# Mixing phases of a hybrid attention and linear-attention backbone: elementwise arithmetic moved from GpSimd to VectorE

## The chip, the cores and the metric

The kernel runs on one core of one Trainium2 chip, in one launch. The metric is the device time of the launch in microseconds (us); the median of a few executions counts. A core has TensorE for matmuls (PE in the profile, its weight loads PEld), VectorE (DVE), ScalarE (ACT), GpSimd (POOL) and SyncE (SP), which here issues all DMAs. Each engine works through its own instructions strictly in the order in which they stand in its queue, and waits on semaphores for the others. TensorE's clock has two levels, 1.2 and 2.4 GHz; the profile shows the granted clock as a share of the upper one.

## What is computed

Two layers over 512 latent tokens and 256 context tokens, width 1024, all in fp32. Cut to what matters here:

```python
h = modulate(rms_norm(x, g_norm1[l]), sh1, sc1)
aq, ak, av, gq, gk, gv, gr, ga, gate_a, gate_b = split_in(h @ w_in[l])
q = rope_2d(rms_norm(aq, q_gain[l]), row, col)      # 16 heads of 64
k = rope_2d(rms_norm(ak, k_gain[l]), row, col)      # 4 key heads
attn = window_attention(q, k, v, kc, vc, sink[l])   # windows of 128, plus all context keys
gf = log_sigmoid(ga @ w_decay + b_decay) / 16       # per direction, cumulated in chunks
o_l = bidir_gla(qg, kg, vg, gf, gb, s_f, s_b)       # 4 heads, decayed key-value states
gla = rms_norm(o_l, gla_gain[l]) * silu(gr)
y = sigmoid(gate_a) * (attn @ w_branch_attn[l]) + sigmoid(gate_b) * (gla @ w_branch_gla[l])
x = x + gt1 * (y @ w_out[l])
x = x + gt2 * squared_relu_mlp(modulate(rms_norm(x, g_norm2[l]), sh2, sc2), w_ff1[l], w_ff2[l])
```

The context tokens run through the same layer with their own modulation, except that the last layer needs no output of theirs.

## The kernel before

**Precision.** Each fp32 operand of a large product is split in two: `hi`, the operand rounded to the matmul type fp32r, and `lo`, the rest. Three matmuls (hi·hi, hi·lo, lo·hi) add up to the product. A split is two instructions: ScalarE makes `hi` (`act`, line 97), then some engine subtracts, `lo = src - hi` (`sub`, line 100). `unit` (line 147) does this for a block of weights that a DMA brought into `raw` (three buffers; `whi` and `wlo` have four each); `split` (line 140) does it for activations. Which engine subtracts is an argument, `lo_eng`, VectorE without it. The helpers `sub`, `mul` and `add` (lines 100, 103, 106) likewise take the engine as their last argument, so most elementwise work shows under these three lines, and only the tile names tell it apart.

**Stages of a layer.** `keys` (norm of the inputs, key and value projections, rotary turn, transposes), `attention`, `gla` (linear attention, four heads one after another), `merge` (gate times branch, added and split into `Y`), `project_out`, and then `mlp`, which the change does not touch. In the trace of before the first layer has its keys at about 65 to 112 us, attention to 480, linear attention to 942, merge to about 972, and the second layer from 1627, 1680, 1960 and 2296 us on.

**Attention.** For each of four groups of heads, each tile of 128 queries and each pair of heads: `queries` projects q into PSUM bank `mq`, normalises (`xn`), multiplies by the cosine and sine tables `rt` (products `r` and `u`, lines 373 and 374), adds and splits (`qh`); `scores` multiplies with the keys into PSUM tile `S`, of which there is one buffer; VectorE reads it with mask and maximum (`p`, `rmax`, line 453), then come the small steps `nm`, `es`, `den` (128x2 each), the exponential on ScalarE and the division of `p`; `values` transposes p (PSUM `pt`, three buffers, copied to `pT`), multiplies by v and splits the result into `ag`. Between these steps the loop puts the products of the merge gates (`gate`) and of the attention branch (`branch`), whose weights come through `unit`.

**Linear attention.** `decay` turns the low-rank product into cumulated decays (`az`, `mz`, a scan into `pf`, subtraction of the middle value `e`, exponentials into `E`); `gla_scan` multiplies keys and queries into `E` and carries the states `st`; `gla_read` makes the outputs, normalises and splits them into `G`. At each head's end `use` fetches the attention branch `ya` from DRAM (`yd`), multiplies it by its gate and sends it back.

**Merge.** `use` fetches gate `sb` and branch `ya` by DMA, computes `yb*sb`, adds `ya`, and splits the sum into `Y`, block by block of 512 or 256 tokens.

**What sets the order.** The program is recorded as it is written, and then a scheduler with a timeline model of its own sorts each engine's queue. The change alters costs and engines, so the scheduler sorts the queues anew, those of TensorE and SyncE too.

Of the kernel before, what the change touches and what calls it, by code (L numbers as in the profile page):

```python
# [59 lines left out]
class Net:  # L60
# [280 lines left out]
    def attn_consts(self, pool, l):  # L341

        nc = self.nc
        self.mask = pool.tile([128, 7, 128], F32, name="mask", bufs=1)
        nc.sync.dma_start(out=self.mask, in_=self.io["cst_mask"])
        rope = self.t2([128, SEQ // 128, 2, HD], "rope")
        nc.sync.dma_start(out=rope, in_=self.io["cst_rope"])
        self.rt = pool.tile([128, 2, SEQ // 128, 2, HD], F32, name="rt", bufs=1)
        for q in range(2):
            g = self.gains[:, q].rearrange("p (o d) -> p o d", o=1).to_broadcast([128, 2 * (SEQ // 128), HD])  # L350
            self.mul(self.rt[:, q].rearrange("p t s d -> p (t s) d"), rope.rearrange("p t s d -> p (t s) d"), g, nc.gpsimd)

    def qk_norm(self, pool, ps, q, t):
# [12 lines left out]
        if t >= SEQ // 128:  # L366
            g = self.gains[:, q].rearrange("p (o d) -> p o d", o=1).to_broadcast([128, 4, HD])
            self.mul(r, xn, g, nc.gpsimd)
            return r
        c = self.rt[:, q, t, 0].rearrange("p (o d) -> p o d", o=1).to_broadcast([128, 4, HD])  # L370
        s = self.rt[:, q, t, 1].rearrange("p (o d) -> p o d", o=1).to_broadcast([128, 4, HD])
        u = pool.tile([128, 4, HD], F32, name="u", tag="u", bufs=1)
        self.mul(r, xn, c, None if q else nc.gpsimd)
        self.mul(u, xn, s, nc.gpsimd if q else None)
        r8 = r.rearrange("p h (a b i) -> p (h a) b i", b=2, i=16)
# [4 lines left out]
    def keys(self, pool, H, us, uv, kT, v, late):  # L380
        nc = self.nc
        for t in CTXS.tiles + LAT.tiles:
            if t == LAT.tiles[0]:
                late()
            ps = self.mm()
            self.tm(ps[:, 0:256], us, H, t)
            r = self.qk_norm(pool, ps, 1, t)
            kd = [self.t2([128, NKV, 2, HD], "kd", F32R) for _ in range(2)]
            rb = r.rearrange("p h (o d) -> p h o d", o=1).to_broadcast([128, NKV, 2, HD])
            self.act(kd[0], rb, ACTF.Copy)  # L390
            self.sub(kd[1], rb, kd[0].bitcast(F32), nc.gpsimd)
            for s in range(2):
                pt = self.pt()
                for g in range(NKV):
                    nc.tensor.transpose(pt[:, g * 128:(g + 1) * 128],
                                        kd[s][:, g].rearrange("p o d -> p (o d)").bitcast(F32), self.ident)
                self.copy(kT[:, :, s, t * 128:(t + 1) * 128], pt.rearrange("p (g t) -> p g t", g=NKV), nc.scalar)
            ps = self.mm()
            self.tm(ps[:, 0:256], uv, H, t)
            self.copy(v[:, t], ps[:, 0:256], nc.scalar)  # L400
# [89 lines left out]
    def attention(self, pool, H, l, kT, v, ya, blocks, gate):  # L490
# [9 lines left out]
        def query(i):  # L500
            nonlocal us
            if i < len(steps):
                g, _, t, _ = steps[i]
                if t == tiles[0]:
                    us = self.panel(w, O_Q + g * 256, lo_eng=self.nc.gpsimd)
                qT[g, t] = self.queries(pool, H, us, t)
# [48 lines left out]

    def gate(self, H, l, off, j, n, sts, use, l0=False):

# [4 lines left out]
        else:  # L562
            src = w[:, c0:c0 + 128].rearrange("(k p) c -> p k c", p=128)
            us = [self.unit(lambda t: self.nc.sync.dma_start(out=t, in_=src), shape=(8, 128), lo_eng=None if l0 else self.nc.gpsimd)]
        for f in range(n):
# [9 lines left out]
    def attn_unit(self, l, g):  # L575
# [3 lines left out]
        def make(c):  # L579
            def loads(t):  # L580
                for s in range(2):
                    self.nc.sync.dma_start(out=t[s * 64:(s + 1) * 64], in_=w[s, :, :, c * 512:(c + 1) * 512])
            return self.unit(loads, shape=(2, 512), lo_eng=self.nc.gpsimd)
        return make
# [85 lines left out]
    def decay(self, st, pool, ga, hd, d, E):  # L670
# [11 lines left out]
        self.act(a, a, ACTF.Ln, bias=1.0)  # L682
        self.sub(m, m, a, nc.gpsimd)
        src, dst = (m, pf) if d == 0 else (m[:, ::-1], pf[:, ::-1])
# [5 lines left out]
        nc.vector.tensor_copy(out=e1, in_=p3[:, :, mid:mid + 1])  # L690
        self.sub(p3, p3, e1.to_broadcast([128, NT, 128]), nc.gpsimd)
        self.act(e2, p3[:, :, last:last + 1], ACTF.Exp, scale=1.0 / 16)
# [39 lines left out]
    def gla_scan(self, st, pool, E, ends, qs, ks, v, prev, full):  # L732
# [7 lines left out]
        for d in range(2):  # L740
            self.mul(E[:, d, 1, tt], ks[:, tt], E[:, d, 1, tt])
            if full:
                self.mul(E[:, d, 0, tt], qs[:, tt], E[:, d, 0, tt], nc.gpsimd)
        S = [{}, {}]
# [31 lines left out]
    def gla_read(self, st, pool, E, S, v, sg, G):  # L776
# [25 lines left out]
        for f in range(2):  # L802
            o = self.t2([128, st.T], "glo")
            self.mul(o, oT[:, f, :st.T], sg[f])
            self.split(G, o, (slice(None), f, slice(st.off, st.off + st.T)), nc.gpsimd)

    def gla(self, pool, H, l, E, yb, sts):
# [5 lines left out]
        def use(j, st, s):  # L813
            tt = slice(st.off, st.off + st.T)
            y = self.t2([128, st.T], "ya1")
            nc.sync.dma_start(out=y, in_=self.yd[:, j, tt])
            self.mul(y, y, s, nc.gpsimd)
            nc.sync.dma_start(out=self.yd[:, j, tt], in_=y)
# [66 lines left out]
    def merge(self, l, H, yb, Y, sts, pool):  # L885
        def use(j, st, s):
# [4 lines left out]
            self.mul(y, y, s)  # L891
            self.add(y, y, a, self.nc.gpsimd)
            self.split(Y, y, (slice(None), j, tt))
# [8 lines left out]
    def gate_early(self, H, l, sts):  # L902
        def keep(j, st, s):
            self.nc.sync.dma_start(out=self.gd[:, j, st.off:st.off + st.T], in_=s)
        return lambda j: self.gate(H, l, O_SB, j, 1, sts, keep, j < 3)

# [300 lines left out]
```

## Time and profile before

| what | value |
|---|---|
| median of three runs | 2745.8 us (2741.91 to 2748.45) |
| the profiled execution: its time | 2742.91 us |
| the profiled execution: span of the core | 2741.1 us |
| TensorE busy | 2579.2 us (94%) |
| weight loads busy | 2267.8 us (83%) |
| VectorE busy | 1634.7 us (60%), 3127 instructions |
| ScalarE busy | 1151.7 us (42%) |
| GpSimd busy | 780.1 us (28%), 574 instructions |
| mean granted clock of TensorE | 0.972 |

The busy times are unions of the instructions' intervals within the span. Matmuls are pipelined, so a busy TensorE is not one at its peak; what can be gained from it without changing its work is the time in which it sits idle, and the time in which it runs at the lower clock.

### The profile page before, as it was taken

What the parts mean: (1) busy time and instruction counts of PE and PEld (TensorE: products, weight loads), DVE (VectorE), ACT (ScalarE), POOL (GpSimd) and SP (SyncE); (2) the same over time, 40 slices, a digit from 0 to 9 for tenths busy, and PEclk for the clock granted to TensorE, in tenths of its full rate; (3) what the DMA queues carried; (4) which work ended last, traced back from release to release, by engine and by line L of the source; (5) the groups of instructions that cost most, each with busy time, mean ns of one, the idle gap of its engine ahead of it and who ended that gap; (6) DMA issues with size and microseconds to landing.
All of it is one profiled execution on the core that took longest, in us unless ns stands there. A gap on an engine that the chain in (4) does not pass through costs nothing. (4 is left out here: it accounts for less than half of the span.)

```text
span 2741.1 us, 43359 instructions
## 1 busy us (share of the span) xinstructions
PE 2579.2 (94%) x17227; PEld 2267.8 (83%) x17227; DVE 1634.7 (60%) x3127; ACT 1151.7 (42%) x2526; POOL 780.1 (28%) x574
## 2 busy tenths in 40 slices
PE   6899999999999898999999988999999998889999
PEld 3888887878878787888888988888888887879898
DVE  4566777534454468644455565787654446677765
ACT  3556554435252334322222245655445334434343
POOL 1413221211120214232223354233122112253444
PEclk7999999999999999999999999999999999999999
DMA  7212123233343433243333241222222225322333
GB/s 252 68 36 72 45 49 100 89 101 93 100 139 90 159 109 93 85 131 107 124 116 123 77 149 47 66 63 68 88 77 85 62 85 177 108 92 90 103 106 111
DMA packets 223838, 269.82 MB, mean 98 GB/s; under 512 B 18480, under 2 KB 185684, under 8 KB 223508
## 3 DMA queue, kind: packets, MB, share of 16 engines
q1 hardware_dynamic: 223636, 267.05, 32.0%
q8 instruction: 135, 2.21, 0.3%
q14 instruction: 67, 0.55, 0.1%
HBM read 244.21 MB, written 22.81 MB: 97 GB/s over the span
## 5 line engine op out<-in xcount | busy, mean ns | idle before, releaser
L97 ACT ACTIVATE whi<-raw 128x1024 fp32r<-128x1024 f32 (+1 forms) x350 | 333.0, 953 | 585.7 <-DMA raw<-in_w_ff 167.2
L920 PE MATMUL mm<-hid,whi 128*128 128x512 f32 (+1 forms) x1664 | 427.3, 347 | 21.0 <-ACT hid L97 10.1
L100 POOL TENSOR_TENSOR wlo<-raw,whi 128x1024 fp32r<-128x1024 f32 x126 | 306.1, 2434 | 321.4 <-ACT whi L97 295.4
L920 PEld LDWEIGHTS mm<-hid,whi 128*128 128x128 f32 x1664 | 290.5, 192 | 72.5 <-issue 11.9
L100 DVE TENSOR_TENSOR wlo<-raw,whi 128x1024 fp32r<-128x1024 f32 (+1 forms) x224 | 238.2, 1064 | 141.2 <-ACT whi L97 137.6
L920 PE MATMUL mm<-hid,wlo 128*128 128x256 f32 (+1 forms) x832 | 281.5, 343 | 0.0
L173 PE MATMUL mm<-H,whi 128*128 128x512 f32 (+1 forms) x760 | 263.0, 347 | 4.8 <-POOL H L100 4.3
L172 PE MATMUL mm<-H,whi 128*128 128x512 f32 (+1 forms) x760 | 264.0, 350 | 2.9 <-ACT H L97 2.1
L174 PE MATMUL mm<-H,wlo 128*128 128x512 f32 (+1 forms) x760 | 261.7, 345 | 0.0
L1065 DVE SCALAR_TENSOR_TENSOR x<-mm,mod,x 128x512 f32<-128x512 f32 (+1 forms) x208 | 126.6, 622 | 125.4 <-PE mm L920 125.1
L920 PE MATMUL mm<-H,whi 128*128 128x384 f32 (+1 forms) x896 | 197.6, 311 | 0.0
L100 POOL TENSOR_TENSOR hid<-c,hid 128x384 fp32r<-128x384 f32 (+1 forms) x112 | 112.4, 1013 | 248.3 <-ACT hid L97 244.0
L920 PEld LDWEIGHTS mm<-hid,wlo 128*128 128x128 f32 x832 | 158.8, 191 | 18.1
L173 PEld LDWEIGHTS mm<-H,whi 128*128 128x128 f32 x760 | 146.6, 193 | 21.0 <-POOL H L100 4.8
L172 PEld LDWEIGHTS mm<-H,whi 128*128 128x128 f32 x760 | 146.4, 194 | 19.9 <-ACT H L97 2.8
L174 PEld LDWEIGHTS mm<-H,wlo 128*128 128x128 f32 x760 | 146.5, 193 | 16.3 <-issue 0.2
L920 PEld LDWEIGHTS mm<-H,whi 128*128 128x128 f32 x896 | 149.8, 190 | 9.4 <-issue 4.9
L920 PE MATMUL mm<-T,whi 128*128 128x384 f32 (+1 forms) x672 | 145.2, 309 | 0.0
L920 PE MATMUL mm<-H,wlo 128*128 128x384 f32 (+1 forms) x448 | 137.5, 309 | 1.1 <-DVE wlo L100 1.1
L97 ACT ACTIVATE p<-p,nm 128x512 f32<-128x512 f32 (+1 forms) x128 | 98.1, 768 | 71.6 <-DVE nm L456 71.6
L453 DVE CUSTOM_DVE_ANT_0 p<-S,mask 128x512 f32<-128x512 f32 (+1 forms) x128 | 96.3, 752 | 46.3 <-PE S L451 44.5
L100 POOL TENSOR_TENSOR mz<-mz,az 128x256 f32<-128x256 f32 (+1 forms) x32 | 36.4, 1137 | 301.3 <-ACT az L97 189.5
(276 smaller groups left out, 6768.3 us busy)
## 6 DMA issues: line engine op xcount, KB each, us to landing
raw<-in_w_ff SPq DMA_DIRECT2D x136, 512.0 KB
raw<-in_w_mod SPq DMA_DIRECT2D x96, 512.0 KB
raw<-in_w_in SPq DMA_DIRECT2D x88, 512.0 KB
raw<-in_w_branch_attn SPq DMA_DIRECT2D x64, 256.0 KB
raw<-in_w_out SPq DMA_DIRECT2D x32, 512.0 KB
raw<-in_w_in SPq DMA_DIRECT2D x32, 256.0 KB
ya<-yd SPq DMA_DIRECT2D x32, 256.0 KB
raw<-in_w_branch_gla SPq DMA_DIRECT2D x16, 512.0 KB
```

The costliest lines, as they stand in the source:

```text
L97: return self.nc.scalar.activation(out=out, in_=in_, func=func, **kw)
L100: (eng or self.nc.vector).tensor_tensor(out=out, in0=a, in1=b, op=ALU.subtract)
L172: nc.tensor.matmul(ps[:, :n], lhsT=wh, rhs=xh, start=(i == 0), stop=False)
L173: nc.tensor.matmul(ps[:, :n], lhsT=wh, rhs=xl, start=False, stop=False)
L174: nc.tensor.matmul(ps[:, :n], lhsT=wl, rhs=xh, start=False, stop=(i == len(ks) - 1))
L453: nc.vector.tensor_tensor_reduce(out=p[:, :nk], in0=S[:, s0:s0 + nk], in1=mask, scale=1.0, scalar=-3e38, op0=ALU.add, op1=ALU.max, accum_o ...
L920: self.nc.tensor.matmul(ps[:, :n], lhsT=a, rhs=b, start=start and i == j == 0, stop=i == last and j == 2, skip_group_check=not start)
L1065: nc.vector.scalar_tensor_tensor(out=xx, in0=ps[:, :n], scalar=self.mod2[:, 5, j, c:c + 1], in1=xx, op0=ALU.mult, op1=ALU.add)
```

## The change

Fourteen places hand their elementwise arithmetic to VectorE instead of GpSimd: the rotary tables and products and the low part of the keys, the low parts of the attention's weight blocks (query panels, attention-branch units, and the gate blocks 3 to 5; gate blocks 0 to 2 were on VectorE already), in `decay` the subtractions on `mz` and `pf`, the product of queries and `E`, the low part of `G`, the product of `ya` and its gate, and the addition in `merge`. The arithmetic is the same. GpSimd keeps its memsets, the low parts of `H` in `norm`, and its work in `mlp`.

```diff
-            self.mul(self.rt[:, q].rearrange("p t s d -> p (t s) d"), rope.rearrange("p t s d -> p (t s) d"), g, nc.gpsimd)
+            self.mul(self.rt[:, q].rearrange("p t s d -> p (t s) d"), rope.rearrange("p t s d -> p (t s) d"), g)
...
-            self.mul(r, xn, g, nc.gpsimd)
+            self.mul(r, xn, g)
...
-        self.mul(r, xn, c, None if q else nc.gpsimd)
-        self.mul(u, xn, s, nc.gpsimd if q else None)
+        self.mul(r, xn, c)
+        self.mul(u, xn, s)
...
-            self.sub(kd[1], rb, kd[0].bitcast(F32), nc.gpsimd)
+            self.sub(kd[1], rb, kd[0].bitcast(F32))
...
-                    us = self.panel(w, O_Q + g * 256, lo_eng=self.nc.gpsimd)
+                    us = self.panel(w, O_Q + g * 256)
...
-            us = [self.unit(lambda t: self.nc.sync.dma_start(out=t, in_=src), shape=(8, 128), lo_eng=None if l0 else self.nc.gpsimd)]
+            us = [self.unit(lambda t: self.nc.sync.dma_start(out=t, in_=src), shape=(8, 128))]
...
-            return self.unit(loads, shape=(2, 512), lo_eng=self.nc.gpsimd)
+            return self.unit(loads, shape=(2, 512))
...
-        self.sub(m, m, a, nc.gpsimd)
+        self.sub(m, m, a)
...
-        self.sub(p3, p3, e1.to_broadcast([128, NT, 128]), nc.gpsimd)
+        self.sub(p3, p3, e1.to_broadcast([128, NT, 128]))
...
-                self.mul(E[:, d, 0, tt], qs[:, tt], E[:, d, 0, tt], nc.gpsimd)
+                self.mul(E[:, d, 0, tt], qs[:, tt], E[:, d, 0, tt])
...
-            self.split(G, o, (slice(None), f, slice(st.off, st.off + st.T)), nc.gpsimd)
+            self.split(G, o, (slice(None), f, slice(st.off, st.off + st.T)))
...
-            self.mul(y, y, s, nc.gpsimd)
+            self.mul(y, y, s)
...
-            self.add(y, y, a, self.nc.gpsimd)
+            self.add(y, y, a)
```

The argument `l0` of `gate`, by which `gate_early` told the first three gate blocks from the others, goes as well.

The queues are sorted anew. The first place is VectorE in the attention of layer 0, in a group of latent queries. Before, in its queue (`p` and `rmax` read `S`, `qh` is the low part of the queries, `ag` that of the attention's output):

```order
L112 COPY pT<-pt 128x512
L100 TENSOR_TENSOR qh<-r,qh 128x4x64
L453 ISA p,rmax<-S,mask 128x640
L453 ISA rmax 128x1
L100 TENSOR_TENSOR ag_2411<-pt,ag_2411 128x128
L456 SCALAR_TENSOR_TENSOR nm<-rmax,nsink 128x2
```

Now, at the same place:

```order
L112 COPY pT<-pt 128x512
L100 TENSOR_TENSOR wlo<-raw,whi 128x1024
L100 TENSOR_TENSOR qh<-r,qh 128x4x64
L453 ISA p,rmax<-S,mask 128x640
L453 ISA rmax 128x1
L100 TENSOR_TENSOR ag_2411<-pt,ag_2411 128x128
```

The low part of a weight block, `wlo`, now stands in VectorE's queue ahead of the queries' low part and of the reading of `S`; before, it stood in GpSimd's.

The second place is VectorE at the border of the first two heads of layer 0's linear attention (`E<-ks` belongs to the next head's scan, `ks` is its key projection taken out of PSUM). Before:

```order
L106 TENSOR_TENSOR mod<-pt,lcol 128x16
L100 TENSOR_TENSOR wlo<-raw,whi 128x1024 x2
L112 COPY mrows<-pt 128x256
L103 TENSOR_TENSOR E<-ks,E 128x256 x2
L112 COPY ks<-mm 128x512
L103 TENSOR_TENSOR E<-ks,E 128x512 x2
```

Now:

```order
L100 TENSOR_TENSOR wlo<-raw,whi 128x1024
L103 TENSOR_TENSOR ya_6509<-ya_6509,sg 128x512
L103 TENSOR_TENSOR ya_6542<-ya_6542,sg 128x256
L100 TENSOR_TENSOR wlo<-raw,whi 128x1024
L103 TENSOR_TENSOR ya_6575<-ya_6575,sg 128x512
L103 TENSOR_TENSOR E<-ks,E 128x256 x2
L103 TENSOR_TENSOR E<-qs,E 128x256 x2
L103 TENSOR_TENSOR ya_6608<-ya_6608,sg 128x256
L112 COPY ks<-mm 128x512
```

The four products of `ya`, each of which waits for a DMA, now stand ahead of the copy that empties a PSUM bank (`ks<-mm`), with the products of queries and `E` between them.

The third place is VectorE in the merge of layer 0. Before:

```order
L103 TENSOR_TENSOR yb<-yb,sb_9875 128x512
L100 TENSOR_TENSOR Y<-yb,Y 128x512
L100 TENSOR_TENSOR Y<-yb,Y 128x256
L103 TENSOR_TENSOR yb<-yb,sg 128x256
L103 TENSOR_TENSOR yb<-yb,sb_9883 128x256
L100 TENSOR_TENSOR Y<-yb,Y 128x512
```

Now:

```order
L103 TENSOR_TENSOR yb<-yb,sb_9875 128x512
L100 TENSOR_TENSOR Y<-yb,Y 128x512
L100 TENSOR_TENSOR Y<-yb,Y 128x256
L106 TENSOR_TENSOR yb<-yb,ya_9877 128x512
L103 TENSOR_TENSOR yb<-yb,sg 128x256
L103 TENSOR_TENSOR yb<-yb,sb_9883 128x256
L103 TENSOR_TENSOR yb<-yb,sb_9891 128x512
L106 TENSOR_TENSOR yb<-yb,ya_9885 128x256
L100 TENSOR_TENSOR Y<-yb,Y 128x512
```

The additions of `ya`, one for each block, now stand between VectorE's own products and low parts.

## Rows read from the trace of the kernel before

**Rows 1.** Busy time by stretch; columns: stretch, length, engines' busy us (instructions), clock, DMA share, GB/s

```profile
112.00:480.00 368.00, 352.99 (x2752) 304.65 (x2752) 254.60 (x688) 197.79 (x539) 81.04 (x53) 1.00 0.22 58
480.00:942.00 462.00, 443.73 (x2807) 380.53 (x2807) 206.81 (x372) 179.82 (x425) 83.48 (x80) 0.99 0.34 105
942.00:972.00 30.00, 22.71 (x127) 19.75 (x127) 27.00 (x31) 15.45 (x29) 19.87 (x15) 0.84 0.75 237
...
1680.00:1960.00 280.00, 262.31 (x2123) 229.49 (x2122) 202.62 (x528) 151.86 (x377) 75.18 (x45) 0.98 0.26 69
1960.00:2296.00 336.00, 323.31 (x1777) 280.48 (x1776) 163.73 (x269) 148.56 (x325) 63.55 (x56) 0.98 0.28 82
2296.00:2326.00 30.00, 25.81 (x143) 22.41 (x142) 26.26 (x27) 13.71 (x20) 14.35 (x8) 0.94 0.64 211
```

**Rows 2.** TensorE's waits, 112 to 480 us: for whom, total us, times, longest

```profile
PE S L448 <- DVE rmax L453: 6.6, 7, 2.0
PE pt L412 <- DVE pT L112: 2.6, 3, 1.5
```

**Rows 3.** TensorE's waits, 1680 to 1960 us

```profile
PE S L448 <- DVE rmax L453: 8.3, 12, 2.4
...
PE pt L479 <- DVE ag L100: 2.1, 2, 1.2
```

**Rows 4.** Timeline of VectorE, 1763 to 1768.5 us: start, length, instruction

```profile
1762.80 1.77 DVE L456 SCALAR_TENSOR_TENSOR nm<-rmax,nsink 128x2 f32<-128x2 f32 x1
1764.60 2.28 DVE L106 TENSOR_TENSOR es<-sink,nm 128x2 f32<-128x2 f32 x1
```

**Rows 5.** Timeline of GpSimd, the same stretch

```profile
1762.16 4.70 POOL L100 TENSOR_TENSOR wlo<-raw,whi 128x1024 fp32r<-128x1024 f32 x2
```

**Rows 6.** Timeline of TensorE, 1767 to 1768 us; in brackets its idle time before

```profile
1767.67 0.66 PE L448 MATMUL S<-kT,qT 128*128 128x384 f32 x2 [2.43 <-DVE rmax L453]
```

**Rows 7.** Groups by form, whole trace: count, busy us, mean ns, idle before, releasers

```profile
L456 DVE SCALAR_TENSOR_TENSOR nm<-rmax,nsink 128x2 f32<-128x2 f32 x80 | 29.4, 368 | 0.9
L100 POOL TENSOR_TENSOR wlo<-raw,whi 128x1024 fp32r<-128x1024 f32 x126 | 306.1, 2434 | 321.4 <-ACT whi L97 295.4 <-ACT es L97 9.8 <-PE pt L479 6.6
```

**Rows 8.** Tile nm: duration ns min/median/max, first and last start

```profile
L456 DVE SCALAR_TENSOR_TENSOR nm<-rmax,nsink x80: 142/154/2356, 130.2 to 1932.4; 128x2 f32<-128x2 f32 x80
```

**Rows 9.** Groups of VectorE by form, 112 to 480 us

```profile
L100 DVE TENSOR_TENSOR wlo<-raw,whi 128x1024 fp32r<-128x1024 f32 x5 | 6.1, 1220 | 4.7 <-ACT whi L97 4.7
```

**Rows 10.** ScalarE's waits, 1680 to 1960 us

```profile
ACT whi L97 <- PE mm L173: 21.9, 16, 3.8
```

**Rows 11.** TensorE's waits, 65 to 112 us

```profile
PE pt L395 <- POOL kd L100: 2.6, 2, 2.4
```

**Rows 12.** Tile kd: duration ns min/median/max

```profile
L100 POOL TENSOR_TENSOR kd<-r,kd x12: 1267/1300/2268, 72.1 to 1676.5; 128x512 fp32r<-128x512 f32 x12
```

**Rows 13.** TensorE's waits, 942 to 972 us

```profile
PE mm L173 <- DVE Y L100: 6.6, 3, 3.7
```

**Rows 14.** TensorE's waits, 2296 to 2326 us

```profile
PE mm L173 <- DVE Y L100: 3.5, 2, 3.0
```

**Rows 15.** Groups of VectorE by form, 942 to 972 us

```profile
L100 DVE TENSOR_TENSOR Y<-yb,Y 128x512 fp32r<-128x512 f32 x6 | 6.2, 1042 | 0.0
L103 DVE TENSOR_TENSOR yb<-yb,sb 128x512 f32<-128x512 f32 x6 | 6.0, 1002 | 1.3 <-DMA sb<-gd 1.3
L100 DVE TENSOR_TENSOR Y<-yb,Y 128x256 fp32r<-128x256 f32 x5 | 5.9, 1171 | 0.0
L103 DVE TENSOR_TENSOR yb<-yb,sb 128x256 f32<-128x256 f32 x6 | 4.9, 814 | 1.0 <-DMA sb<-gd 1.0
```

**Rows 16.** Tile yb: duration ns min/median/max, first and last start, forms

```profile
L106 POOL TENSOR_TENSOR yb<-yb,ya x24: 742/1436/2203, 945.7 to 2319.7; 128x512 f32<-128x512 f32 x16, 128x256 f32<-128x256 f32 x8
...
L100 DVE TENSOR_TENSOR Y<-yb,Y x24: 411/688/1774, 949.1 to 2322.6; 128x512 fp32r<-128x512 f32 x16, 128x256 fp32r<-128x256 f32 x8
```

**Rows 17.** GpSimd's waits, 480 to 942 us

```profile
POOL ya L103 <- DMA ya<-yd: 18.5, 6, 5.9
```

More of the change, by code (lines that the diff above doesn't have):

```diff
@@ L554, in sigmoid, with gate @@
         self.act(out, out, ACTF.Exp, scale=-1.0)
-    def gate(self, H, l, off, j, n, sts, use, l0=False):
+    def gate(self, H, l, off, j, n, sts, use):
         w = self.io["w_in"][l]
@@ L904, in keep @@
             self.nc.sync.dma_start(out=self.gd[:, j, st.off:st.off + st.T], in_=s)
-        return lambda j: self.gate(H, l, O_SB, j, 1, sts, keep, j < 3)
+        return lambda j: self.gate(H, l, O_SB, j, 1, sts, keep)
     def relu2(self, ps, n, hid, t0):
```

## The prediction

> **What bounds the kernel now.** I read the busy table by stretch first. In the two attentions and the two linear attentions TensorE is busy 353 of 368, 444 of 462, 262 of 280 and 323 of 336 us [rows 1]. So TensorE is the bound, and moving elementwise work can win or lose only in its idle time, 60 us over these four stretches, and in the two merges, where VectorE is busy 27.0 and 26.3 of 30 us and TensorE waits [rows 1]. There VectorE is the bound. The clock is at its upper level almost everywhere in attention (1.00 and 0.98), and falls to a mean of 0.84 in the first merge [rows 1].
>
> Then I read who ends TensorE's waits. In attention it is VectorE: 6.6 us for the reading of the scores, 2.6 for a transposed copy [rows 2], and 8.3 and 2.1 in the second layer [rows 3]. What VectorE was doing then is in the timelines: at 1762.8 us the 128x2 step `nm` takes 1.77 us and the next, `es`, 2.28 us [rows 4], while the median of `nm` is 154 ns [rows 8]. GpSimd began two weight splits at 1762.16 us that ended 4.70 us later, at 1766.86 [rows 5], and `es` ended at 1766.88, with its work. Only then was `S` read, and TensorE had waited 2.43 us [rows 6]. A VectorE instruction that finds GpSimd in a 2.43 us split [rows 7] does not run slower in proportion; it ends when GpSimd ends. Over all 80 `nm` the mean is 368 ns against that median [rows 7, 8]: 80 x 0.214 = 17 us of VectorE's time from this one small step. The largest waits of the attentions have this picture. The Trainium skill has it as a rule ("SBUF — State Buffer", section "SBUF: two separate sides"): GpSimd and a VectorE instruction with two SBUF inputs take a shared port pair as an exclusive lock for a whole instruction, so the later one waits it out. The trace agrees, with the 2.28 us step.
>
> **The change part by part.**
>
> *Prices.* An elementwise instruction of two SBUF inputs takes VectorE 0.41 us for 256 columns and 0.69 for 512 where nothing disturbs it, the minimum and the median of `Y` [rows 16], and 1.22 us for a weight block of 1024 [rows 9]. GpSimd takes 2.43 for that block [rows 7] and a median of 1.44 for the additions of the merge [rows 16].
>
> *Attention (A).* GpSimd's 53 and 45 instructions here [rows 1] are 25 weight splits in each layer, 24 and 16 products of 256 columns, and four memsets each. VectorE gets 25 x 1.22 + 24 x 0.41 = 40 us in layer 0 and 25 x 1.22 + 16 x 0.41 = 37 in layer 1, and would be busy 295 of 368 and 240 of 280 us even if no stretched step became shorter; the 17 us of `nm` alone should come off that. It stays under TensorE's share, but in layer 1 not by much. What goes: waits of 6.6 + 2.6 + 8.3 + 2.1 = 19.6 us [rows 2, 3], so far as GpSimd causes them. What is late next: a split still holds VectorE, for 1.22 us instead of 2.43, and in the new order it can stand right ahead of a reading of `S`. So half the blocking stays. I take half, **-9.8 us**; the ends are 0 and -19.6.
>
> *Keys (B).* The last tile's keys wait for GpSimd's low part: TensorE loses 2.6 us to it [rows 11]. That part takes 1.30 us, once 2.27 [rows 12], and 0.69 on VectorE. `r` and `u` ran side by side on two engines, stretching each other, and now follow one another at 0.41 each, which is about even. The longest wait of 2.4 us should lose the difference 2.27 - 0.69 = 1.6; the second layer's keys are built alike. I take 1.5 for each layer, **-3 us**, between 0 and -5 (the 2.6 us of both layers).
>
> *Linear attention (D).* VectorE gets 40 instructions of 512 columns in each layer and 40 and 16 of 256: 44 and 34 us, which bring it to 251 of 462 and 198 of 336 us [rows 1]. TensorE's work covers that. What is new is a wait: the four products of `ya` at each head's end wait for DMAs, for which GpSimd sat idle 18.5 us in six waits, 5.9 at the longest [rows 17], hurting nobody. Now these waits stand in VectorE's queue, ahead of the next head's key and query products and of the copy that empties a PSUM bank; the scores of that head and TensorE's next projection wait for those. But SyncE issues these loads right behind the weight blocks whose splits stand ahead of them in VectorE's queue, so VectorE arrives late too. Between the two I take **0**, from -3 (the decay chain loses a hop between engines at each of two steps) to +9 (half of the 18.5).
>
> *Merge (C).* VectorE is the bound here, so its sum counts. It gets 8 x 0.69 + 8 x 0.41 = 8.8 us of additions in layer 0 and 8 x 0.69 = 5.5 in layer 1. What it loses is the stretch that GpSimd's additions cause: against 0.688 and 0.411 [rows 16] the four groups cost 6 x 0.354 + 6 x 0.314 + 5 x 0.760 + 6 x 0.403 = 10.2 us too much [rows 15]. So the load falls by 1.4 us although work comes in; layer 1 I count as even. Besides, each block's chain is shorter by 1.44 - 0.69 = 0.75 us [rows 16], which shows in the five waits of 6.6 + 3.5 = 10.1 us [rows 13, 14]: 5 x 0.75 = 3.7. With 1 us back from the clock (0.84 and 0.94 over 30 us are 4.8 and 1.8 us lost, [rows 1]) I take **-6 us**, between +4 (nothing of the stretch goes: 8.8 + 5.5 = 14.3 us of new work, less all of the 10.1 us of waits) and -13 (no new work shows: the 10.1 us of waits and half of the clock's 6.6).
>
> The Trainium skill has a rule that speaks against this edit ("Perfetto Trace Analysis", section "Optimizing Scalar/DVE Operations"): where VectorE is saturated, giving some of its work to another engine, even GpSimd, may pay; it adds that between those two it may not help. The merge is the one saturated place; by the first half of it C would be a loss.
>
> *Moved queues.* SyncE's loads and TensorE's products are sorted anew in the same phases, with the same number of DMAs and matmuls; a stored `ya` now waits for VectorE instead of GpSimd. I cost this at 0, inside D's ends.
>
> **Sum.** -9.8 - 3 - 6 + 0 = -18.8 us. Against the profiled execution's 2742.9 us that is 2724.1. The median of the runs lies 2.9 us above that execution, so I predict **2727 us**.
>
> **The rivals.**
>
> *Nothing left over.* VectorE's queue takes A back (0), D costs its +9, B and C bring -9: **2746 us**. For it: VectorE at up to 240 of 280 us in layer 1, and sorted by a model that is not the chip. Against it: the stretched steps leave.
>
> *VectorE's queue stalls TensorE (slower).* A split on VectorE waits for ScalarE's high part, and that waits for a free weight buffer, which TensorE's earlier matmuls release: 16 times in layer 1, 21.9 us [rows 10]. On GpSimd only the split stood behind that. On VectorE the readings of `S` stand behind it: TensorE finishes with the buffer, goes on to the scores, and finds VectorE still in the split. The five splits that VectorE has in layer 0's attention waited 4.7 us [rows 9]. If this costs TensorE a split's 1.22 us at 24 places of the 50 (the 16 of layer 1 and half as many in layer 0), it is 29 us, no gain in A, -9 from B and C: **2766 us**. It decides from some 8 places on, if A brings nothing, and from 15 if A brings its 9.8.
>
> *The whole of it goes.* If GpSimd is the only thing that makes VectorE late, A is -19.6, B -5, C -13, D -3: -40.6, **2705 us**. For it: the instant in which `es` ends with GpSimd's split. Against it: some waits have no stretched step ahead. The lock rule of the Trainium skill's page "SBUF — State Buffer" would give this, if the new splits cost VectorE nothing in time; nothing in this trace shows that.
>
> *The change does not do what it says* can be left out: in the new order GpSimd has no such instruction left in these phases, though `norm` keeps its low parts there.
>
> **How the numbers follow.** Forecast 0.60, nothing left 0.14, slower 0.14, the whole 0.12. The forecast with its spread is 2715 to 2740; the range of 8 in 10 goes down to the whole gain and up past no change, **2704 to 2753**, and leaves the slower rival out. A measurement can tell about 0.2% (5.5 us) from no change: faster, under 2740.3, is the forecast less its upper edge and the whole, 0.70; within, 0.16; slower 0.14.
>
> **What would show it.** Right: in the changed profile `nm` has a mean near its median of 154 ns; TensorE's waits for `rmax` fall to about half of 14.9 us; the forms of the merge have 0.69 and 0.41 us and TensorE's waits for `Y` are under 7 us; the linear attentions keep their 462 and 336 us within 3. Wrong: VectorE idle before `wlo` for ScalarE's `whi` by tens of us in attention with longer waits of TensorE for `rmax` (the slower rival), or a wait of VectorE for `ya`'s DMA followed by one of TensorE for `ks` (D mis-sized).

## The result, and the profile after

| | before | after |
|---|---|---|
| median (lowest to highest) | 2744.61 us (2741.63 to 2748.45) | 2719.08 us (2718.03 to 2721.53) |
| ratio, 95% interval | | 0.9909 (0.9894 to 0.9923) |
| profiled span | 2741.1 us | 2719.7 us |

So the change brings 25.0 us (21 to 29). The forecast was 2727, with 2704 to 2753 as its range. A repetition in another set of runs gave 2717.15 and a ratio of 0.9911 (0.9897 to 0.9925).

The first part of the page of the changed kernel (busy us, share of the span, instructions):

```profile
PE 2573.1 (95%) x17227; PEld 2263.8 (83%) x17227; DVE 1697.6 (62%) x3409; ACT 1152.5 (42%) x2526; POOL 403.8 (15%) x292
```

GpSimd lost 376 us of work, and VectorE, which took all of it over, is busy only 63 us longer. The busy table over the stretches of [rows 1] shows where that comes from (of the five busy times the third is VectorE's, the fifth GpSimd's; the stretches are the same in us, and so shifted against the program by up to 20 us in layer 1):

```profile
112.00:480.00 368.00, 355.13 (x2742) 306.66 (x2742) 261.18 (x736) 197.39 (x537) 1.61 (x4) 0.99 0.22 58
480.00:942.00 462.00, 442.07 (x2808) 378.02 (x2808) 234.30 (x453) 180.24 (x427) 0.00 (x0) 1.00 0.34 105
942.00:972.00 30.00, 23.34 (x140) 20.58 (x139) 26.14 (x51) 15.14 (x30) 0.00 (x0) 0.89 0.73 233
1680.00:1960.00 280.00, 269.76 (x2189) 237.12 (x2188) 213.92 (x587) 160.66 (x395) 1.63 (x4) 0.99 0.29 74
```

In layer 0's attention the prediction had added 40 us to VectorE's 254.6 and come to 295; it is 261.2. Some 33 us of stretched steps left as the new work came in, not only the 17 us of `nm`, which were all that the prediction had counted for the whole kernel. In the first merge VectorE has 20 instructions more and is busy 26.1 us instead of 27.0.

The tile `nm`, to be read against [rows 8] (duration in ns, minimum, median, maximum):

```profile
L456 DVE SCALAR_TENSOR_TENSOR nm<-rmax,nsink x80: 149/154/163, 126.0 to 1914.6; 128x2 f32<-128x2 f32 x80
```

The median has stayed, and the tail of up to 2356 ns is gone. In VectorE's timeline of layer 1's attention (start, length, instruction) a weight split now stands right ahead of `nm` and `es`, and neither of them is longer than its median; in [rows 4, 5] they had 1.77 and 2.28 us beside GpSimd's splits:

```profile
1775.58 1.22 DVE L100 TENSOR_TENSOR wlo<-raw,whi 128x1024 fp32r<-128x1024 f32 x1
1776.72 0.15 DVE L456 SCALAR_TENSOR_TENSOR nm<-rmax,nsink 128x2 f32<-128x2 f32 x1
1776.90 0.16 DVE L106 TENSOR_TENSOR es<-sink,nm 128x2 f32<-128x2 f32 x1
```

TensorE's waits for the reading of the scores, in layer 0's attention (112 to 480 us) and layer 1's (1680 to 1960 us), against the 6.6 and 8.3 us of [rows 2, 3] (total, times, longest):

```profile
PE S L448 <- DVE rmax L453: 2.5, 4, 0.9
PE S L448 <- DVE rmax L453: 3.6, 5, 1.2
```

The keys: TensorE's wait for the high part, which ScalarE makes, in 65 to 112 us of the kernel before, where it stands beside the 2.6 us of [rows 11]; TensorE's only wait there now; and the tile of the keys' low part, now on VectorE (against [rows 12]). The 2.6 us are gone, and the wait for the high part is 0.6 us longer:

```profile
PE pt L395 <- ACT kd L97: 3.5, 2, 2.5
...
PE pt L395 <- ACT kd L97: 4.1, 1, 4.1
```

```profile
L100 DVE TENSOR_TENSOR kd<-r,kd x12: 678/692/695, 70.0 to 1670.1; 128x512 fp32r<-128x512 f32 x12
```

The merges: two groups of VectorE by form in 942 to 972 us (against [rows 15]), and TensorE's waits in 942 to 972 and 2296 to 2326 us (against [rows 13, 14]):

```profile
L100 DVE TENSOR_TENSOR Y<-yb,Y 128x512 fp32r<-128x512 f32 x8 | 5.5, 688 | 0.0
L100 DVE TENSOR_TENSOR Y<-yb,Y 128x256 fp32r<-128x256 f32 x8 | 3.4, 422 | 0.0
```

```profile
PE mm L173 <- DVE Y L100: 6.0, 5, 3.3
PE mm L172 <- ACT Y L97: 0.4, 1, 0.4
...
PE mm L173 <- DVE Y L100: 1.4, 1, 1.4
```

The forms fell to 0.69 and 0.42 us, as forecast. The waits did not follow: 10.1 us before and 7.4 now, with 1.7 us of waits for ScalarE's half of `Y` beside them (0.4 in the first merge, 1.3 just ahead of 2296 us).

What the prediction feared is there as well. VectorE's waits in the two attentions (112 to 480, 1680 to 1960 us) and in layer 0's linear attention (480 to 942 us):

```profile
DVE wlo L100 <- ACT whi L97: 11.6, 9, 5.5
...
DVE wlo L100 <- ACT whi L97: 10.2, 9, 2.3
...
DVE ya L103 <- DMA ya<-yd: 12.6, 8, 3.3
```

### The profile page after: what moved, and what is told of

Its sections match the earlier page's. It is cut to its first block, busy times and chain, and to the rows that moved or that the text cites. A ratio compares the mean times of both kernels' runs of the same rounds, so it can differ in the third digit from the quotient of the medians.

```text
span 2719.7 us, 43217 instructions
## 1 busy us (share of the span) xinstructions
PE 2573.1 (95%) x17227; PEld 2263.8 (83%) x17227; DVE 1697.6 (62%) x3409; ACT 1152.5 (42%) x2526; POOL 403.8 (15%) x292
## 5 line engine op out<-in xcount | busy, mean ns | idle before, releaser
L100 DVE TENSOR_TENSOR wlo<-raw,whi 128x1024 fp32r<-128x1024 f32 (+1 forms) x278 | 296.7, 1068 | 155.0 <-ACT whi L97 152.0
L100 POOL TENSOR_TENSOR H<-xr,H 128x256 fp32r<-128x256 f32 x33 | 38.8, 1185 | 1106.5 <-ACT H L97 704.1
L100 POOL TENSOR_TENSOR wlo<-raw,whi 128x1024 fp32r<-128x1024 f32 x72 | 176.0, 2447 | 115.1 <-ACT whi L97 114.7
L991 DVE SCALAR_TENSOR_TENSOR c<-c 128x384 f32<-128x384 f32 (+1 forms) x112 | 96.3, 865 | 30.8 <-ACT c L97 28.6
```

Of the source, the lines that this page charges most:

```text
L100: (eng or self.nc.vector).tensor_tensor(out=out, in0=a, in1=b, op=ALU.subtract)
L991: nc.vector.scalar_tensor_tensor(out=c, in0=c, scalar=0.0, in1=c, op0=ALU.max, op1=ALU.mult)
```

## Where the time went, by stage

A table from the traces alone: each matmul was weighted with the median duration of its form over all traces, and each trace was asked when TensorE had done as much of that work as in the first trace of the kernel before at the end of a stage. The numbers are us gained (-) or lost (+) within the stage; the small differences ahead of the keys are left out.

| trace | keys 0 | attention 0 | linear 0 | merge, projection 0 | feed-forward 0 | keys 1 | attention 1 | linear 1 | rest |
|---|---|---|---|---|---|---|---|---|---|
| before, again | -1.1 | 1.2 | -1.8 | -0.8 | -0.6 | -1.2 | 2.3 | 0.1 | -0.2 |
| after | -3.3 | 2.1 | -0.4 | -3.1 | 0.0 | -3.2 | -9.7 | -3.9 | 0.5 |
| after, again | -3.3 | 0.7 | 3.2 | -3.3 | -2.0 | -1.8 | -10.9 | -5.6 | -1.4 |
| A alone | -2.1 | -4.7 | 0.5 | -3.4 | 0.6 | -3.1 | -8.3 | 0.0 | -1.8 |
| A and B | -3.2 | 1.8 | -0.6 | -4.1 | -0.8 | -3.1 | -10.7 | 0.5 | 2.2 |
| C alone | 0.3 | -0.3 | -0.5 | -3.8 | -0.7 | 1.0 | 1.8 | -3.8 | -1.0 |
| D alone | 0.3 | -0.1 | 5.1 | -3.5 | 0.2 | -0.9 | 3.5 | -3.2 | -0.4 |
| all on VectorE | -2.6 | -0.6 | 0.6 | -3.6 | -18.4 | -3.2 | -11.0 | -5.7 | -16.8 |
| `H` and `b` on VectorE | -2.7 | -0.5 | 3.2 | -2.6 | -12.2 | -2.9 | -10.9 | -5.6 | -4.6 |
| B alone | -2.4 | -1.9 | 2.3 | -3.7 | -0.9 | -1.1 | 5.8 | -1.6 | 0.2 |
| the change without A | -2.2 | -1.8 | -1.5 | -2.2 | -1.0 | -2.8 | 6.7 | -6.4 | 0.8 |
| subtractions doubled | -3.4 | 1.8 | -1.6 | -2.3 | -0.1 | 5.2 | 20.7 | -5.1 | -2.7 |

The two traces of the same kernel before differ by up to 2.3 us in a stage, and the two of the changed kernel by up to 3.6, so a number below 3 says little. The large one of the change is layer 1's attention; without A it is not only gone, but the stage loses 6.7 us, as B alone loses 5.8 there. The trace of C alone is of its fastest execution, 9 us under its median, so its row flatters it.

## The experiments

**The changed kernel again**, as the base of the two that follow.

> The changed kernel itself, unaltered, as the base of this set. Every theory: 2719 us within 3, ratio 0.991. What it is to tell besides: the changed kernel's first trace has two stretches of 3.4 us at the lower clock in layer 0's attention (at 130 and 396 us) that the kernel before had not, and lacks two of those that it had in layer 1's. If these belong to the new order of the queues, they stand at the same places again; if they come by chance, they stand elsewhere, and then the division of the gain among the stages is uncertain by 2 to 3 us for each.

Measured: 2717.15 us. Of the two stretches of lower clock in layer 0's attention, the one at 130 us stands there again (at 129 us, and in the run of A and B too), and the one at 396 us doesn't (it does in the run of A and B, at 395 us). So the first belongs to the new order of the queues; the gain of single stages is uncertain by some 3 us.

**GpSimd does the low parts of layer 1's attention a second time.** The tile `ya` has 256 columns for context tokens, which layer 1 does not use; GpSimd's result goes there and is read by nobody.

```diff
         self.sub(lo[idx], raw[idx], hi[idx].bitcast(F32), lo_eng)
+        if dup and self.spare is not None:
+            f = lambda t: t.rearrange("p a b -> p (a b)").rearrange("p (a b) -> p a b", b=256)
+            self.sub(self.spare, f(raw), f(hi).bitcast(F32), self.nc.gpsimd)
```

> The changed kernel, in which GpSimd computes in layer 1's attention the low part of each of the 30 weight blocks a second time, into a tile that nobody reads; VectorE's own instructions and those of TensorE and ScalarE stand in exactly the same order as in the changed kernel. Theory (a two-input instruction of GpSimd holds VectorE's two-input instructions until it ends): the steps nm and es of layer 1 are stretched again, up to 2.4 us, with a mean of nm in layer 1 of 300 to 450 ns against 154; TensorE's waits for rmax there go from 3.6 us back to 7 to 9, and the kernel is 4 to 10 us slower than the changed one (2723 to 2729). Rival (the gain came from the low parts being ready earlier, or from the new order of the queues): nm stays at 154 ns and the time within 2 us of the changed kernel's.

Measured: 2760.10 us (2754.92 to 2763.26), ratio to the kernel before 1.0059 (1.0046 to 1.0073). Useless work on an idle engine costs 43 us against the 2717.15 of the same set, with the queues of VectorE, TensorE and ScalarE in the same order as in the changed kernel. By stage, 5.2 against -3.2 and -1.8 is in layer 1's keys, where the first four doubled subtractions stand, and 20.7 against -9.7 and -10.9 in its attention. So with GpSimd at work the new order has no gain to show, which speaks strongly against it as the cause, and the steps of VectorE are held again; but I had expected 4 to 10 us. (Lines are shifted here: `nm` is L460, the splits L101.) VectorE, in 1690 to 1960 us by form, and TensorE's first wait in 1690 to 1990:

```profile
L101 DVE TENSOR_TENSOR wlo<-raw,whi 128x1024 fp32r<-128x1024 f32 x27 | 45.4, 1682 | 8.1 <-ACT whi L98 8.1
L460 DVE SCALAR_TENSOR_TENSOR nm<-rmax,nsink 128x2 f32<-128x2 f32 x32 | 11.2, 351 | 0.1
...
PE S L452 <- DVE rmax L457: 13.6, 8, 3.8
```

Why more than in the kernel before, where `nm` had the same tail, is in the two timelines, GpSimd's and VectorE's:

```profile
1771.58 5.88 POOL L101 TENSOR_TENSOR ya<-raw,whi 128x1024 f32<-128x1024 f32 x2 [3.76 <-ACT whi L98]
1791.66 3.38 POOL L101 TENSOR_TENSOR ya<-raw,whi 128x1024 f32<-128x1024 f32 x1 [14.20 <-ACT whi L98]
```

```profile
1773.05 1.99 DVE L460 SCALAR_TENSOR_TENSOR nm<-rmax,nsink 128x2 f32<-128x2 f32 x1
...
1775.56 2.98 DVE L101 TENSOR_TENSOR wlo<-raw,whi 128x1024 fp32r<-128x1024 f32 x1
...
1791.56 1.23 DVE L101 TENSOR_TENSOR wlo<-raw,whi 128x1024 fp32r<-128x1024 f32 x1 [0.32 <-ACT whi L98]
1792.71 2.35 DVE L107 TENSOR_TENSOR den<-den,es 128x2 f32<-128x2 f32 x1
```

Both engines' splits wait for the same `whi`, so they start together. Where VectorE's is first (1791.56), GpSimd's takes 3.38 us, its own 2.4 and most of VectorE's 1.23 before it, and then holds VectorE's next step, `den`, until 1795.06. Where GpSimd's is first, VectorE's split takes 2.98. The two pairs are laid end to end, and of the 30 doubled blocks 13 subtractions of GpSimd took 3.20 us or more and nine of VectorE 2.6 or more. A part of the 43 us is the clock, which falls to 0.92 to 0.96 in the thirds of this attention, where the changed kernel has 1.00 (by these shares some 14 us, an estimate). Another part may be the buffers: the useless work also reads `raw` and `whi`, and in 1660 to 1990 us SyncE's loads waited 15.5 us for it, in seven waits, and ScalarE's high part once, 3.8 us. How the 43 us divide among the hold, the clock and the buffers is not shown.

**GpSimd copies the block instead**, one input in place of two (1.17 us in place of 2.77).

```diff
-            self.sub(self.spare, f(raw), f(hi).bitcast(F32), self.nc.gpsimd)
+            self.nc.gpsimd.tensor_copy(out=self.spare, in_=f(raw))
```

> As the run before, but GpSimd copies the raw block (one input) in place of subtracting (two inputs). If what holds VectorE is that GpSimd works at all on these blocks, the stretches of nm, es and of the division of p come back as with the subtraction, in proportion to the copy's duration. If it needs two inputs on GpSimd's side, nm stays near 154 ns and the time within 2 us of the changed kernel's. I hold the first for the likelier (0.6): 2721 to 2728 us.

Measured: 2722.61 us (2718.18 to 2727.55), 5.5 us over the changed kernel of the same set. `nm` in layer 1:

```profile
L460 DVE SCALAR_TENSOR_TENSOR nm<-rmax,nsink x32: 145/151/997, 1695.0 to 1918.6; 128x2 f32<-128x2 f32 x32
```

A one-input instruction of GpSimd holds VectorE too, for as long as it takes: four `nm` took 0.61 to 1.00 us, and each ended within 0.02 us of a copy's end. The runs of the two kernels overlap (2716.71 to 2720.18 and 2718.18 to 2727.55), so the 5.5 us are rough.

**The change without its part A.**

```diff
-                    us = self.panel(w, O_Q + g * 256)
+                    us = self.panel(w, O_Q + g * 256, lo_eng=self.nc.gpsimd)
...
-            return self.unit(loads, shape=(2, 512))
+            return self.unit(loads, shape=(2, 512), lo_eng=self.nc.gpsimd)
```

(and the gate's blocks 3 to 5 likewise)

> The change without its part A: the low parts of attention's weight blocks stay on GpSimd, all else goes to VectorE. Theory (A is worth about 10 us, the other parts 9 to 15): 2729 to 2736 us, ratio 0.995 to 0.997; TensorE's waits for rmax in the two attentions near the 14.9 us of before. Rival (the new order of the queues brought the gain, not the missing splits): 2719 to 2724.

Measured: 2733.30 us (2729.67 to 2740.68), ratio 0.9969 (0.9957 to 0.9980). `nm` has its tail again. The tile, and TensorE's waits in layer 1's attention (1700 to 1960 us):

```profile
L456 DVE SCALAR_TENSOR_TENSOR nm<-rmax,nsink x80: 144/152/2197, 127.4 to 1927.5; 128x2 f32<-128x2 f32 x80
...
PE S L448 <- DVE rmax L453: 6.1, 4, 2.4
PE pt L485 <- DVE pT L112: 5.5, 5, 2.4
PE mm L172 <- DVE ya L106: 1.7, 5, 0.5
PE pt L479 <- DVE ag L100: 1.7, 2, 1.2
```

A is worth 16 us on top of the other parts, more than the 10 of the theory, and by stage they lie in layer 1's attention (6.7 against -9.7 and -10.9). The waits for `rmax`, however, came back only to 9.7 us in the two attentions (1.9 and 7.8), not to the 14.9 that I had expected; in layer 1's those for `pT` grew instead, 5.5 us against 2.2 in the first trace of the kernel before.

**Each part alone**, the edits being the lines of the change sorted by part: A the three lines on weight blocks (`panel`, `gate`, `attn_unit`), B the rotary tables, `r`, `u` and `kd`, C the addition in `merge`, D the five lines on `mz`, `pf`, `E`, `G` and `ya`.

> Part A alone: the kernel before with the low parts of attention's weight blocks on VectorE, all else as before. The run without A was 16 us slower than the changed kernel (2733.3 against 2717.2). If A's worth doesn't depend on the other parts: 2727 us, between 2723 and 2731, and the gain lies in layer 1's attention (some 14 us) with none in layer 0's. If A pays only together with the other parts (the rotary products of the queries, which stay on GpSimd here, still hold VectorE): 2733 to 2738.

> Part B alone: rotary tables and products and the low part of the keys on VectorE, which takes the products of the queries in the two attentions along. By the prediction's B: 3 us, so 2740 (2738 to 2743), with the wait of TensorE for kd on GpSimd gone (2.6 us in each layer before) and 2 us less idle TensorE in each keys stage. Rival: the wait for kd only passes on to the high part on ScalarE, as the changed kernel's trace has it (one wait of 4.1 us), and the time stays within 1 us of 2743.

> Part C alone: the additions of the merge on VectorE. By the prediction's C: 6 us, so 2737 (2734 to 2740); by the changed kernel's trace, where the first merge ends 3.6 us earlier and the second 1.7, 2738. Rival (VectorE is the bound of the merges, so more work in it costs): 2744 to 2748. In the trace the form Y of 512 columns should fall from 1.04 to about 0.69 us in the first merge.

> Part D alone: the linear attention's five kinds of products and subtractions on VectorE. By the prediction's D: 0, so 2743 (2740 to 2746). Rival (the products of ya, which wait for their DMA, stop VectorE's queue): 2748 to 2752, with VectorE idle before ya by over 15 us and waits of TensorE for ks or E that the kernel before does not have.

| kernel | median us | ratio, 95% interval | us against 2744.6 | prediction |
|---|---|---|---|---|
| A alone | 2721.48 | 0.9919 (0.9906 to 0.9932) | -22 (-26 to -19) | -9.8 |
| B alone | 2738.02 | 0.9981 (0.9971 to 0.9991) | -5 (-8 to -2) | -3 |
| C alone | 2744.02 | 1.0002 (0.9990 to 1.0014) | +1 (-3 to +4) | -6 |
| D alone | 2742.78 | 0.9997 (0.9987 to 1.0006) | -1 (-4 to +2) | 0 |

A alone does nearly all of it, and a little more than the 2723 to 2731 us that I had expected. The tail of `nm` is gone with A alone:

```profile
L456 DVE SCALAR_TENSOR_TENSOR nm<-rmax,nsink x80: 144/153/316, 126.2 to 1911.3; 128x2 f32<-128x2 f32 x80
```

In A alone the wait for the low part of the keys is shorter too, though it is still GpSimd's. TensorE's waits for it in 62 to 114 and 1630 to 1690 us, and, from the first trace of the kernel before, what GpSimd did ahead of the last keys but one of layer 0:

```profile
PE pt L395 <- POOL kd L100: 0.9, 2, 0.5
...
PE pt L395 <- POOL kd L100: 0.8, 2, 0.5
```

```profile
99.10 2.40 POOL L100 TENSOR_TENSOR wlo<-raw,whi 128x1024 fp32r<-128x1024 f32 x1 [0.53 <-ACT whi L97]
101.45 2.27 POOL L100 TENSOR_TENSOR kd<-r,kd 128x512 fp32r<-128x512 f32 x1
```

The low part of the first query panel stands in GpSimd's queue right ahead of the keys' and delays them. A part of the wait only passes on to ScalarE's high part. TensorE's waits for that, in 62 to 114 us of A alone and of B alone, against the 3.5 us of before:

```profile
PE pt L395 <- ACT kd L97: 4.0, 1, 4.0
...
PE pt L395 <- ACT kd L97: 5.2, 1, 5.2
```

So of 6.1 us of waits for the keys in layer 0, 4.9 are left in A alone, 5.2 in B alone and 4.1 in the changed kernel. The expectation had 14 us for A in layer 1's attention and none in layer 0's; its one trace has 8.3 and 4.7 there, and the trace of A and B has its gain in layer 1's alone. Why B shifts it, and why B alone loses 5.8 us in layer 1's attention, is open.

C alone stayed at 2744.0, where I had expected 2734 to 2740; that is the low end of its rival, by which more work on a bound VectorE costs time. TensorE's waits of its first merge (938 to 976 us) add up to nearly what they were. The wait for `Y` on VectorE is 5.6 us, against 6.9 in the same stretch of the kernel before (8.6 in its second trace), and there is one for ScalarE's half of `Y`:

```profile
PE mm L173 <- DVE Y L100: 5.6, 5, 3.3
PE mm L172 <- ACT Y L97: 1.1, 2, 0.6
```

The additions' 8.8 us fill most of what the stretch leaves free: VectorE is busy 29.3 of these 38 us, against 30.9. That this sum sets the merge's end is my reading of it, and no run isolates it. A alone, whose additions stay on GpSimd, has waits of 4.8 and 1.1 us in the same stretch, so the shorter ones of the changed kernel are not C's work.

D alone has VectorE's new waits for the DMA of `ya` (14.9 us in layer 0's linear attention), and its time is that of the kernel before: TensorE has no wait for VectorE's copy `ks`.

**A and B together.**

> Parts A and B together, without the merge and the linear attention (C and D). A alone gave 2721.5, the whole change 2717.2 to 2719.1. Theory (C and D bring nothing in time): 2717 to 2720. Rival (they bring what the prediction gave C, 6 us, once A is done): 2723 to 2726. Third: B costs in attention as it does alone there (its run has 3.7 us more idle TensorE in layer 1's attention), also with A: 2722 to 2725.

Measured: 2723.51 us (2722.32 to 2724.43), ratio 0.9924 (0.9911 to 0.9936). The theory's 2717 to 2720 is missed; the rival and the third both hold this time, and do not part here. On top of A, B brings nothing that these runs can tell; of the 5 us that it has alone 3.5 are in the keys stages by its trace, where A alone gains 5.2. C and D on top of both bring 4 us (ratios 0.9924 and 0.9909), whose intervals overlap. The table by stage puts a gain in layer 1's linear attention in every trace that has C or D (-3.2 to -6.4) and hardly any where both are missing (0.5 to -1.6). In D alone and in the changed kernel TensorE's waits there for `sgr` are 3.1 us against 4.0, and those for `a` 0.0 and 0.8 against 2.1, some 2 to 3 us. What C does there is open.

**A second trace of the kernel before.**

> The kernel before, unaltered, for a second trace of it: 2744 us within 5. Every variant run so far, those that leave the first merge's neighbours alone among them, has the stretch from 942 to 1050 us some 3.5 us shorter than the first trace of the kernel before. If that trace had an unlucky stretch of the lower clock there (13.7 us from 962.6 on), the second trace has less of it and the stretch is shorter by about 3 us; if it belongs to the kernel, it stands there again.

Measured: 2741.02 us. It has 10.2 us of lower clock in the first merge where the first trace had 13.7, and is 0.8 us shorter between 942 and 1050 us. So the stretch belongs to the kernel, and not to one unlucky execution. Why the variants that leave the merge as it is are also some 3.5 us shorter there is open.

**One step further: no arithmetic on GpSimd at all.** The norm's low parts, the weight splits of `w_ff2`, the low parts of `hid`, the sums `s` and the additions `b` that rebuild `H` ahead of the feed-forward part go to VectorE as well.

```diff
-                self.split(H, xr, (slice(None), k, tt), nc.gpsimd)
+                self.split(H, xr, (slice(None), k, tt))
...
-            self.split(h, c, (slice(None), slice(t0, t0 + n)), nc.gpsimd)
+            self.split(h, c, (slice(None), slice(t0, t0 + n)))
...
-                        us = self.panel(io["w_ff2"][l], p * 256, rows=(ch * CH, (ch + 1) * CH), lo_eng=nc.gpsimd)
+                        us = self.panel(io["w_ff2"][l], p * 256, rows=(ch * CH, (ch + 1) * CH))
```

(and the lines of `s` and `b` likewise)

> One step further than the change: the norm's low parts and the feed-forward part's arithmetic (72 weight splits, 112 low parts of hid, and the sums for the seven products) go to VectorE too, so that GpSimd does only memsets. There VectorE is busy 591 of 958 us in the changed kernel and gets some 72 x 1.22 + 112 x 0.48 + 60 x 0.6 = 178 us, less the 108 us by which its own steps are stretched there: 661 of 958, a load as in attention. Theory (what GpSimd's instructions hold is the only cost that counts): TensorE's waits there that end with GpSimd (2.7 + 1.5 + 1.5 us) or with VectorE late (some 5 us) go, 2711 to 2717. Rival (there the stretched steps wait for nobody, TensorE has 912 busy of 958 us and its idle time lies at the borders of the stages): within 2 us of the changed kernel's 2717 to 2719.

Measured: 2682.36 us (2680.38 to 2685.74), ratio 0.9776 (0.9763 to 0.9790). Both expectations were far off: it is 36 us faster than the change, the fastest kernel of the study. The table by stage puts 18.4 us into layer 0's feed-forward part and most of the rest into layer 1's. The busy table for its first 60 us, of the changed kernel (second trace) and of this one:

```profile
1050.00:1110.00 60.00, 49.76 (x307) 44.60 (x306) 53.63 (x79) 23.62 (x53) 35.51 (x24) 0.86 0.17 54
```

```profile
1050.00:1110.00 60.00, 59.52 (x403) 51.57 (x401) 54.93 (x116) 25.69 (x57) 0.00 (x0) 1.00 0.25 80
```

VectorE is busy nine tenths of it in both, once for 79 instructions and once for 116. It was the bound there, with steps held like this (0.43 us and 0.56 us in the kernel without GpSimd):

```profile
1071.74 2.62 DVE L103 TENSOR_TENSOR r<-r 128x256 f32<-128x256 f32 x1
1074.28 1.36 DVE L100 TENSOR_TENSOR b<-b,b 128x384 f32<-128x384 f32 x1
```

I had added up the waits of TensorE that the view ends with GpSimd, and called the rest borders of the stages. The rest was VectorE, and VectorE was late because it was held. The lower clock goes with the bubble (0.86 against 1.00).

**A part of that step**: `H` and the additions `b` only.

> A part of the run before that gave 2682.4: the changed kernel, and the norm's low parts H and the 64 additions b that rebuild H at the start of the feed-forward part go to VectorE, while the 72 weight splits of w_ff2, the low parts of hid and the sums s stay on GpSimd. In the changed kernel VectorE's steps of 0.55 us there take 1.36, those of 0.41 up to 2.62, from 1067 to 1087 us, beside additions b of 1.1 to 1.3 us and splits of 2.5 to 2.7 us on GpSimd. Theory (the bubble comes from the additions b, both as a chain of two engines and as what holds VectorE): most of the 36 us, 2685 to 2697. Rival (the weight splits and hid hold VectorE and cost it): 2708 to 2718. In between both have a part.

Measured: 2702.05 us (2699.03 to 2705.14), ratio 0.9859 (0.9843 to 0.9875); against the changed kernel's 0.9909 that is 14 us, of the 36. So `H` with the additions has a part, and what stayed on GpSimd (the weight splits, `hid` and `s`, not told apart) has another, as the expectation's last sentence allows; in layer 0 the former is 12 us of 18 (by stage), in layer 1 the latter has more: there TensorE still waits 5.7 us for `hid` and 2.7 for GpSimd's `wlo`.

## Why the prediction was right, and where it was off

- **The mechanism** was right, and the doubled work shows it, not only the comparison of before and after: the hold comes back with GpSimd's instructions alone, while the queues of VectorE, TensorE and ScalarE stay as they are. The Trainium skill's rule ("SBUF — State Buffer", section "SBUF: two separate sides"), an exclusive lock held for a whole instruction, agrees with the 3.38 and 2.98 us of the pairs that met.
- **A, attention** (-9.8): in the two stages it brought -7.6 and -10.2 us in the changed kernel's two traces and -13.0 in A alone's, and the waits for `rmax` fell from 14.9 to 6.1, somewhat more than half. But the term stopped at attention's border. A alone is 22 us, 5 of them in the two keys stages, where the first query panel's split delayed the keys. The rest, some 4 us, lies in stages in which other variants gain as much, and stays open.
- **B, keys** (-3): the size fits B alone, -2.4 and -1.1 us in the two stages. But the term left out two things. A alone brings as much there (-2.1 and -3.1), by the queue ahead of `kd`, and the two overlap (-6.5 and -5.1 for both stages in the changed kernel); and B alone loses 5.8 us in layer 1's attention. A part of the wait passed on to ScalarE's high part (3.5 us before, 4.1 now, in layer 0).
- **C, merge** (-6): wrong. C alone brought nothing (+1 us, -3 to +4). The forms did what was forecast, but of the 10.1 us of waits 9.1 are left in the changed kernel, those for ScalarE's half of `Y` included. The failed step is the 3.7 us for shorter chains of blocks: if VectorE's sum sets the end, as I read it, a shorter chain of one block gives nothing. The Trainium skill says that relieving a saturated VectorE, even through GpSimd, may pay, and that between these two it might not ("Perfetto Trace Analysis", section "Optimizing Scalar/DVE Operations"); here the second half holds, as the addition costs the same on either engine.
- **D, linear attention** (0): right in sum. VectorE's waits for `ya` came (12.6 us in layer 0) and cost nothing that the total shows (-1 us for D alone, -4 to +2). Layer 1 gained 3.9 and 5.6 us in the changed kernel, past the term's lower end, but C alone has that gain too.
- **The rivals.** *VectorE's queue stalls TensorE*: its sign came, 21.8 us of waits for `whi` in attention, but not its price. I had written that this sign with longer waits for `rmax` would show the rival; the second half is what decides. *Nothing left over* rested on VectorE at 240 of 280 us; it was at 213.9, since the held time leaves as the work comes. *The whole of it goes* gave 2705, and the result lies between it and the forecast.
- **The sum**: -25 us measured, -18.8 forecast. A was too small by 12, C too large by 6 to 7; the errors partly cancelled, and the parts overlap (A and B bring 22 and 5 alone and 21 together), so it is partly luck that the total came this near.

## What to carry to other kernels

Where a step of two SBUF inputs on VectorE has a tail of many times its median, look at what GpSimd does in that instant, and count all of VectorE's held time, not that of one tile: it comes off VectorE's load when GpSimd's work moves over, so that the move costs less than the moved work's sum. A low share of GpSimd in a stage (22 and 27% in the two attentions here) does not make it harmless, and a stage in which VectorE looks saturated may be one in which it is held. Ask of every queue that an instruction leaves what stood behind it there, also across the border of a stage, and follow the finding to the stages that the change leaves alone: the larger gain was there.

## What the runs showed of the hardware that I had not expected

- The hold works in both directions: GpSimd's subtraction of 1024 columns takes 2.4 us alone and 3.38 behind VectorE's of 1.23; VectorE's takes 2.98 behind GpSimd's.
- Work that nobody needs, 30 such subtractions on an otherwise idle GpSimd, cost the kernel 43 us, about half of their own 30 x 2.77 us (what they cost through the buffers and the clock included).
- VectorE's reading of the scores, whose first input is in PSUM, was not held in that run: its tile `p` there has 671 to 826 ns, against 676 to 827 in the changed kernel (second trace). In the kernel before it never took more than 827 either, although 30 of its 128 instances began while GpSimd was in an instruction.
- Two whole tiles as inputs are not needed for the hold: the division of `p` by `den` (one tile and one column, both in SBUF) has a median of 486 ns and a longest of 2710 in the kernel before, and 484 and 556 in the changed one.
